# Seven products for eight in the first gate and up block too, with h scaled by x's norm factor

## The chip, the cores and the metric

The kernel runs on one core of one Trainium2 chip. The time is the device time of one execution in microseconds; the median of three runs is given. TensorE multiplies; VectorE (DVE), ScalarE (ACT) and GpSimd (POOL) do the rest; SyncE (SP) and POOL start the DMA transfers. Each engine has a queue of its own, which it works off in the written order.

## The reference

One layer of a hybrid block on 256 rows of width 2048, all in float32:

```
xn = rms_norm(x, norm1_g)
q, k, v, ga, gg = split(xn @ w_in)                 # w_in: 2048 x 5120
att = diff_attention(rope(rms_norm(q)), rope(rms_norm(k)), v)
u   = silu(layer_norm(conv(ga * sigmoid(gg))))
h   = x + concat(att, u) @ w_out                   # w_out: 2048 x 2048
hn  = rms_norm(h, norm2_g)
y   = h + (silu(hn @ w_gate) * (hn @ w_up)) @ w_down   # 2048 x 5632, 5632 x 2048
```

where `rms_norm(t, g) = t * rsqrt(mean(t*t) + 1e-6) * g`.

## The kernel before

**Products.** The 256 rows are two halves of 128 (`m`, `NM = 2`). Every float32 operand is split into a high part (rounded, float32r) and a low part (the rest), and a product is three matmuls: high x high, low x high, high x low. Weights come in chunks of two k-tiles by 512 columns (`raw`, 512 KB). ScalarE rounds a chunk to `whi` (L348), VectorE subtracts to `wlo` (L357); for a chunk marked `by_dma` ScalarE writes `-raw` (L351) and a POOL transfer adds the weights to it (L352). A plain chunk is twelve matmuls of 128x128 by 128x512.

**Seven for eight.** From the second gate and up block on, and in w_down, half of the k-tiles go through a Strassen-like scheme: the two row halves and a pair of weights form a 2x2 problem that takes seven products instead of eight. Such a unit ("s") multiplies one of seven sums of input rows (`forms`: `fhi`, `flo`) with one of seven sums of weights. Its weights are a tile `wb` of 1 MB (`load_pair`); VectorE makes three sums (`pair_sums`, L1064 to L1066), ScalarE rounds (`round_raw` L1071, `round_pair` L1075 and L1076) and VectorE makes the low parts (`split_pair`, L1080 and L1081). A unit "s" is 21 matmuls into the banks Q1 to Q3. The other half of the k-tiles is plain: units "g" (gate) and "u" (up) of twelve matmuls; a capital letter means `by_dma`. A block of 512 columns of gate and up is four "s", four "g" and four "u", in the order of `ORDER` or `FIRST`. Behind the last "s" `bank_sums` puts the products together, and behind the last unit `block_done` finishes the block.

**The first block.** Gate and up block 0 is made of plain chunks (`block`, sixteen chunks, 192 matmuls), with `silu_done` and `up_done` at its end; its inputs are `hT`, h transposed and times norm2's gain, without the factor `rstd2`, which is applied to the sums. During it `make_forms` spreads `rstd2` over a tile (`rep`, two transposes L1000, `rb`), multiplies the transposed rows `hn` by it, and makes the plain parts (`chi`, `clo`) and the forms for all later blocks.

**w_out.** Four column blocks n of 512. The last k-tiles of blocks 0, 1 and 2 are done one after the other, four chunks each, then all eight chunks of block 3, then gate and up block 0. `out_done(n)` adds the result to h (L850), starts the transfer of h to the output, transposes h (L862), scales by the gain (`hn`, L867), splits to `hT` and takes the sum of squares (L524). Blocks 0, 1 and 3 accumulate in the four `acc` banks, block 2 in two `aux` banks; in a Strassen unit Q1, Q6, Q7, Q5 are `acc` and the rest `aux`.

**Order of the work.** The queues' order is written out by the program. `run_chunks` goes through the chunks; ahead of chunk t it issues the splits, sums, roundings and loads of later chunks (splits up to three chunks ahead, sums five, roundings three or four, loads nine; before the first Strassen unit two and three). Generators such as `out_done` and `make_forms` go on by one `yield` at each `resume()`, of which a plain chunk has two and an "s" unit four:

```
until("part", part_of, t + 1 + LO_AHEAD)
...
until("sums", sums_of, t + 1 + ahead - (...), may=may_sum)
...
chunks[t]["multiply"](chunks[t])
```

Pools: `pre`, `once` and `small` hold what is needed until h is done; the pool `ffn` is opened in their place afterwards.

Of the kernel before, what the change touches and what calls it, by code (L numbers as in the profile page):

```python
# [13 lines left out]
F32 = mybir.dt.float32  # L14
# [70 lines left out]
FIRST = "gugusGsUsGsU"  # L85
# [32 lines left out]
def tile_block(  # L118
# [12 lines left out]
    prestack = ExitStack()  # L131
    pre = prestack.enter_context(tc.tile_pool(name="pre", bufs=2))
    once = prestack.enter_context(tc.tile_pool(name="once", bufs=1))
    small = prestack.enter_context(tc.tile_pool(name="small", bufs=4))
# [4 lines left out]
    h = [pre.tile([P, D], F32, tag=f"h{m}", name=f"h{m}", bufs=1) for m in range(NM)]  # L139

    rstd2 = [const.tile([P, 1], F32, tag=f"rstd2_{m}", name=f"rstd2_{m}") for m in range(NM)]
# [3 lines left out]
    neghalf = once.tile([P, 8], F32, tag="neghalf", name="neghalf")  # L145
# [10 lines left out]
    cols = once.tile([P, NR], F32, tag="cols", name="cols")  # L156
# [8 lines left out]
    head = pre.tile([P, NK * N], F32, tag="lod", name="head", bufs=1)[:, : NR + S]  # L165
# [54 lines left out]
    def rsqrt_mean(dst, ss, n, eps):  # L220

        k = dst.shape[-1]
        t = small.tile([P, 8], F32, tag="rsq", name="rsq")
        pool.tensor_scalar(t[:, :k], ss, 1.0 / n, eps, ALU.mult, ALU.add)
        pool.tensor_tensor(dst, t[:, :k], neghalf[:, :k], ALU.pow)

# [114 lines left out]
    def minus_chunk(c):  # L341
        c["lo"] = c["view"](pre.tile([P, NK * N], F32R, tag="lod", name="lod", bufs=1))
        act.activation(c["lo"], c["raw"], AF.Copy, scale=-1.0)
        pool.dma_start(out=c["lo"].rearrange("p k n -> p (k n)"), in_=c["src"].bitcast(F32R), accum_op=ALU.add)
# [174 lines left out]
    rstd1 = [once.tile([P, 1], F32, tag=f"rstd1_{m}", name=f"rstd1_{m}") for m in range(NM)]  # L519
    ss1 = [small.tile([P, D // N], F32, tag=f"ss1_{m}", name=f"ss1_{m}", bufs=1) for m in range(NM)]  # L520

    def square_sum(src, accum, **kw):
        junk = pre.tile([P, N], F32, tag="junk", name="junk", bufs=1)
        act.activation(junk[:, : src.shape[-1]], src, AF.Square, accum_out=accum, **kw)  # L524
# [14 lines left out]
    def x_rest():  # L539
# [6 lines left out]
        for m in range(NM):  # L546
            ss = small.tile([P, 1], F32, tag="ss1", name="ss1")
            dve.tensor_reduce(ss, ss1[m], AX.X, ALU.add)
            rsqrt_mean(rstd1[m], ss, D, EPS)
# [63 lines left out]
    def conv_back(b):  # L613
# [37 lines left out]
        for b in range(2):  # L651
            for t in range(NB // 2):
# [6 lines left out]
                for j in range(2):  # L659
# [3 lines left out]
                    hi = pre.tile([P, S], F32R, tag="mchi", name=f"mchi{ct}", bufs=NCT)  # L663
                    lo = pre.tile([P, S], F32R, tag="mclo", name=f"mclo{ct}", bufs=NCT)
# [137 lines left out]
    def attend_values(hd):  # L802
# [26 lines left out]
        for e in range(2):  # L829
# [3 lines left out]
            pre.tile([P, S], F32R, tag=t, name=t, bufs=4) for t in ("mahi", "malo")) for e in range(2)]  # L833
# [10 lines left out]
    hn = []  # L844
    ss2 = [once.tile([P, 4], F32, tag=f"ss2_{m}", name=f"ss2_{m}") for m in range(NM)]

    def out_done(n, ps):
# [5 lines left out]
        if n == 2:  # L853
            held[0] -= NM
        yield
        for t in range(0, N // P, 2):
# [3 lines left out]
            for i in range(2):  # L860
                for m in range(NM):
                    pe.transpose(pt[:, i, m * P : (m + 1) * P], h[m][:, (k + i) * P : (k + i + 1) * P], ident)  # L862
            if k % HK == 0:
                hn.append(early.tile([P, HK, S], F32, tag="wb", name="hn"))
            rows = hn[k // HK][:, k % HK : k % HK + 2, :]
            for i in range(2):
                act.activation(rows[:, i, :], pt[:, i, :], AF.Copy, scale=col("g2", k + i))  # L867
            hi, lo = lhs_two("h", k)
            act.copy(hi, rows)
            dve.tensor_tensor(lo, rows, hi.bitcast(F32), ALU.subtract)  # L870
            for i in range(2):
                hT[k + i] = (hi[:, i, :], lo[:, i, :])
            yield
        for m in range(NM):
            square_sum(h[m][:, cs], ss2[m][:, n : n + 1])
        if n == D // N - 1:
            yield
            for m in range(NM):
                ss = small.tile([P, 1], F32, tag="ssh", name="ssh")
                dve.tensor_reduce(ss, ss2[m], AX.X, ALU.add)  # L880
                rsqrt_mean(rstd2[m], ss, D, EPS)
            yield
            yield
            prestack.close()
            ffn["pool"] = fp = ctx.enter_context(tc.tile_pool(name="ffn", bufs=1))
            spare_lhs.extend(fp.tile([P, SPARE, 2, S], F32R, tag=f"a{x}", name=f"a{x}") for x in ("hi", "lo"))
            start(make_forms())


    ffn = {}  # L890
    actT = {}
    sil = {}

    def silu_done(ps):
        yield
        for m in range(NM):
            sil[m] = ffn["pool"].tile([P, N], F32, tag=f"sum{m}", name="sil")
            act.activation(sil[m], ps[m], AF.Silu, scale=rstd2[m])

    def up_done(j, ps):  # L900
        fp = ffn["pool"]
        aa = []
        for m in range(NM):
            a = fp.tile([P, N], F32, tag=f"sum{2 + m}", name="a")
            dve.scalar_tensor_tensor(a, ps[m], rstd2[m], sil[m], ALU.mult, ALU.mult)
            aa.append(a)
        yield from lag(2)
        place(0)
        pts = []
        for t in range(NB // 2):  # L910
            pts.append(acc_ps.tile([P, 2, S], F32, tag="acc", name="ps_a"))
            transpose_two(pts[t], aa, t)
        for t in range(NB // 2):
            act.copy(down[0]["at"][j, t][0], pts[t])
        yield
        for t in range(NB // 2):
            hi, lo = down[0]["at"][j, t]
            dve.tensor_tensor(lo, pts[t], hi.bitcast(F32), ALU.subtract)
            down[0]["ready"].add((j, t))
# [10 lines left out]
    def place(g):  # L930
# [6 lines left out]
        free += [tuple(a[:, i] for a in spare_lhs) for i in range(SPARE)]  # L937
        assert len(free) >= len(twos)
# [5 lines left out]
    def transposed(j, aa):  # L944
# [4 lines left out]
        for t in range(N // P // 2):  # L949
# [4 lines left out]
            else:  # L954
                hi, lo = d["at"][j, t]
                if j == FF // N - 1:
                    a = ffn["pool"].tile([P, 2, S], F32, tag=f"sum{2 * t}", name="ac")
# [8 lines left out]
    def pair_forms(j, t, pt):  # L966

        fp = ffn["pool"]
# [22 lines left out]
    def make_forms():  # L991
        fp = ffn["pool"]
        load_pair(chunks[pair_at[0]])
        rep = fp.tile([P, S], F32, tag="sum1", name="rep")
        for m in range(NM):
            act.activation(rep[:, m * P : (m + 1) * P], ident, AF.Identity, bias=rstd2[m], scale=0.0)
        yield from lag(2)
        ps = aux_ps.tile([P, N], F32, tag="aux", name="ps_r")
        for m in range(NM):
            pe.transpose(ps[:, m * P : (m + 1) * P], rep[:, m * P : (m + 1) * P], ident)  # L1000
        yield
        rb = fp.tile([P, S], F32, tag="sum2", name="rb")
        act.copy(rb, ps[:, :S])
        yield
        for i in range(2):
            for k in range(0, HK, 4):
                t = hn[i][:, k : k + 4, :]
                dve.tensor_tensor(t, t, rb.unsqueeze(1).to_broadcast([P, 4, S]), ALU.mult)
                yield from lag(1 if i == 0 else 2)

        nr = HK - NS
        chi = fp.tile([P, 2 * nr, S], F32R, tag="chi", name="chi")
        clo = fp.tile([P, 2 * nr, S], F32R, tag="clo", name="clo")
        for i in range(2):
            act.copy(chi[:, i * nr : (i + 1) * nr], hn[i][:, NS:])
        yield
        pair_sums(chunks[pair_at[0]])
        yield
        for i in range(2):
            dve.tensor_tensor(clo[:, i * nr : (i + 1) * nr], hn[i][:, NS:],  # L1020
                              chi[:, i * nr : (i + 1) * nr].bitcast(F32), ALU.subtract)
            yield from lag(2 - i)
        forms.update(plain={k: (chi[:, i, :], clo[:, i, :]) for i, k in enumerate(REST)})
        a11, a21 = (hn[0][:, :NS, m * P : (m + 1) * P] for m in range(NM))
        a12, a22 = (hn[1][:, :NS, m * P : (m + 1) * P] for m in range(NM))
        fhi = fp.tile([P, 7, NS, P], F32R, tag="fhi", name="fhi")
        flo = fp.tile([P, 7, NS, P], F32R, tag="flo", name="flo")
        f = fp.tile([P, 7, NS, P], F32, tag="wh", name="sums", bufs=2)[:, :4]
# [9 lines left out]
        for i, a in ((0, a11), (1, a12)):  # L1038
            dve.tensor_tensor(flo[:, i], a, fhi[:, i].bitcast(F32), ALU.subtract)
        yield  # L1040
        act.copy(fhi[:, 3:], f)
        round_raw(chunks[pair_at[0]])
        dve.scalar_tensor_tensor(flo[:, 2], a22, -1.0, fhi[:, 2].bitcast(F32), ALU.mult, ALU.subtract)
        yield from lag(2)
        dve.tensor_tensor(flo[:, 3:], f, fhi[:, 3:].bitcast(F32), ALU.subtract)
        forms.update(hi=fhi, lo=flo)

    def load_pair(c):
        if "b" in c:
            return  # L1050
        queue = sp
        if c is chunks[pair_at[0]]:
            c["b"] = ffn["pool"].tile([P, 7, N], F32, tag="wl", name="wb0", bufs=2)[:, :4]
            queue = pool
        else:
            c["b"] = early.tile([P, 4, N], F32, tag="wb", name="wb")
        src = weights([(w, k, col, N) for w, col in c["sides"] for k in c["ks"]])
        queue.dma_start(out=c["b"].rearrange("p k n -> p (k n)"), in_=src)

    def pair_sums(c):  # L1060

        b = c["b"]
        c["t"] = t = ffn["pool"].tile([P, 3, N], F32, tag="wt", name="wt")
# [4 lines left out]
    def round_raw(c):  # L1068
        if "hi" not in c:
            c["hi"] = ffn["pool"].tile([P, 7, N], F32R, tag="wh", name="wh", bufs=2)  # L1070
# [280 lines left out]
```

## Time and profile before

| | |
|---|---|
| three runs | 1035.57, 1035.73, 1035.88 us |
| median | 1035.73 us |
| span of the profiled execution, first to last instruction | 1033.9 us, 1.8 us less than the median of the runs |
| TensorE busy | 1025.0 us (99%) |
| VectorE, ScalarE, POOL busy | 882.0 (85%), 697.5 (67%), 157.1 us (15%) |
| mean granted TensorE clock | 0.999 |
| moved by DMA | 258.05 MB, 250 GB/s on average |

The profiled execution's own time is its span and what lies around it; no figure of its own is given beside the three runs. Times in a timeline are microseconds from the start of the span. Each row has start, length, engine, line of the kernel, operation, "out <- in" with shapes, a count, and in brackets the idle time of the engine before it with what ended it. A matmul's length overlaps the next one's.

### The profile page before, as it was taken

The numbers are of one execution on the slowest core, as the hardware profiler recorded it, in microseconds if no ns is written. First come the engines' busy times: TensorE is split into PE (matmuls) and PEld (weight loads), VectorE is DVE, ScalarE is ACT, GpSimd is POOL, SyncE is SP. The second block draws the span as 40 slices with busy tenths as digits, with TensorE's granted clock in tenths as the row PEclk, the third lists the DMA queues.
The fourth block names the chain that finished last, engine by engine and source line by source line (L and its number), as shares of the span: only waits on it lengthen the run. The fifth ranks groups of instructions, "written<-read, shape, count | busy, mean of one in ns | idle before, by whom it ended". The sixth has DMA issues, their size and how long they took to land.

```text
span 1033.9 us, 13145 instructions
## 1 busy us (share of the span) xinstructions
PE 1025.0 (99%) x4635; PEld 847.3 (82%) x4635; DVE 882.0 (85%) x1111; ACT 697.5 (67%) x933; POOL 157.1 (15%) x198
## 2 busy tenths in 40 slices
PE   9999999999999999999999999999999999999998
PEld 7888887888888888788888888888888888888887
DVE  6699889897646699999989879999898887998984
ACT  7855567857756577787665757776767576767761
POOL 0050332411100101011002120110110221101122
PEclk9999999999999999999999999999999999999999
DMA  9968675676566668798899997987979999889896
GB/s 362 314 202 248 224 208 184 191 217 184 156 211 224 230 241 237 246 325 233 264 291 246 313 267 260 308 249 243 310 239 278 271 263 330 228 257 301 242 259 130
DMA packets 65345, 258.05 MB, mean 250 GB/s; under 512 B 7296, under 2 KB 8576, under 8 KB 57344
## 3 DMA queue, kind: packets, MB, share of 16 engines
q1 hardware_dynamic: 48080, 201.08, 53.6%
q0 software_dynamic: 16768, 55.58, 28.8%
q8 instruction: 36, 0.59, 0.2%
q10 hardware_dynamic: 432, 0.55, 0.2%
q14 instruction: 29, 0.24, 0.1%
HBM read 248.80 MB, written 8.39 MB: 249 GB/s over the span
## 4 chain that ended last, share of the span: by engine, by line
PE 90%; DVE 5%; issue 2%; ACT 2%; POOL 1%; DMA 0%; DVEq 0%
PE q L1120 20%; PE acc L393 11%; PE acc L387 11%; PE acc L388 11%; PE q L1125 10%; PE q L1098 8%; PE q L1100 8%; PE q L1099 8%; DVE wl L1081 1%; PE ps_a L925 1%; DVE wt L1064 1%; DVE wl L1080 1%; ACT whi L348 1%; PE ps_s L734 1%; PE ps_o L812 1%
## 5 line engine op out<-in xcount | busy, mean ns | idle before, releaser
L348 ACT CAST whi<-raw 128x1024 fp32r<-128x1024 f32 (+1 forms) x254 | 261.9, 1041 | 66.0 <-PE acc L388 44.2
L357 DVE TENSOR_TENSOR wlo<-raw,whi 128x1024 fp32r<-128x1024 f32 (+1 forms) x166 | 199.6, 1210 | 41.8 <-ACT whi L348 41.4
L1071 ACT CAST wh<-wb 128x1536 fp32r<-128x1536 f32 x62 | 91.9, 1483 | 117.0 <-issue 67.4
L1080 DVE TENSOR_TENSOR wl<-wb,wh 128x2048 fp32r<-128x2048 f32 x62 | 141.9, 2288 | 33.9 <-ACT wh L1075 33.6
L387 PE MATMUL acc<-whi,lhi 128*128 128x512 f32 x416 | 164.2, 395 | 0.4 <-ACT whi L348 0.4
L388 PE MATMUL acc<-whi,llo 128*128 128x512 f32 x416 | 162.4, 391 | 0.0
L352 POOL DMA_DIRECT2D wlo<-in_wts_dram x74 | 65.2, 881 | 526.6 <-ACT wlo L351 408.1
L1098 PE MATMUL q<-wh,fhi 128*128 128x512 f32 x280 | 109.2, 390 | 1.5 <-DVE sum L1223 1.5
L1100 PE MATMUL q<-wl,fhi 128*128 128x512 f32 x280 | 109.0, 389 | 0.0
L1099 PE MATMUL q<-wh,flo 128*128 128x512 f32 x280 | 109.0, 389 | 0.0
L1081 DVE TENSOR_TENSOR wl<-wt,wh 128x1536 fp32r<-128x1536 f32 x62 | 108.6, 1752 | 0.0
L599 DVE SCALAR_TENSOR_TENSOR y<-upad,cw,y 128x256 f32<-128x256 f32 x240 | 100.7, 484 | 3.4 <-ACT y L592 3.4
L393 PE MATMUL acc<-wlo,lhi 128*128 128x512 f32 x368 | 100.8, 395 | 1.1 <-DVE wlo L357 1.1
L387 PEld LDWEIGHTS acc<-whi,lhi 128*128 128x128 f32 x416 | 78.2, 188 | 17.1 <-ACT whi L348 1.1
L1076 ACT CAST wh<-wt 128x1536 fp32r<-128x1536 f32 x62 | 91.7, 1480 | 0.0
L388 PEld LDWEIGHTS acc<-whi,llo 128*128 128x128 f32 x416 | 78.2, 188 | 16.0
L1125 PE MATMUL q<-wlo,chi 128*128 128x512 f32 x320 | 86.9, 394 | 0.0
L1120 PE MATMUL q<-whi,chi 128*128 128x512 f32 x320 | 85.8, 390 | 0.0
L1120 PE MATMUL q<-whi,clo 128*128 128x512 f32 x320 | 85.7, 390 | 0.0
L393 PEld LDWEIGHTS acc<-wlo,lhi 128*128 128x128 f32 x368 | 68.4, 188 | 15.3 <-DVE wlo L357 1.5
L351 ACT ACTIVATE wlo<-raw 128x1024 fp32r<-128x1024 f32 x74 | 78.0, 1054 | 0.0
L1064 DVE TENSOR_TENSOR wt<-wb 128x1024 f32<-128x1024 f32 x62 | 75.7, 1221 | 1.4 <-DMA wb<-in_wts_dram 0.9
(229 smaller groups left out, 1740.1 us busy)
## 6 DMA issues: line engine op xcount, KB each, us to landing
raw<-in_wts_dram SPq DMA_DIRECT2D x250, 512.0 KB, 6.1
wb<-in_wts_dram SPq DMA_DIRECT2D x61, 1024.0 KB, 7.4
wlo<-in_wts_dram POOLq DMA_DIRECT2D x74, 512.0 KB, 9.2
lod<-in_wts_dram POOLq DMA_DIRECT2D x14, 512.0 KB, 5.9
out_dram<-sum POOLq DMA_DIRECT2D x22, 256.0 KB, 5.9
h<-in_x_dram SPq DMA_DIRECT2D x4, 512.0 KB, 9.6
out_dram<-h POOLq DMA_DIRECT2D x8, 256.0 KB, 3.8
xt<-in_xt_dram SPq DMA_DIRECT2D x6, 256.0 KB, 6.5
```

Of the source, the lines that this page charges most:

```text
L348: act.copy(c["hi"], c["raw"])
L357: dve.tensor_tensor(c["lo"], c["raw"], c["hi"].bitcast(F32), ALU.subtract)
L387: pe.matmul(ps[m], xhi[:, ms], hi[:, j, :], start=c["first"] and j == 0, stop=False)
L388: pe.matmul(ps[m], xlo[:, ms], hi[:, j, :], start=False, stop=False)
L393: pe.matmul(ps[m], xhi[:, ms], lo[:, j, :], start=False, stop=c["last"] and j == nk - 1)
L1080: dve.tensor_tensor(c["lo"][:, 3:], c["b"], c["hi"][:, 3:].bitcast(F32), ALU.subtract)
L1081: dve.tensor_tensor(c["lo"][:, :3], c["t"], c["hi"][:, :3].bitcast(F32), ALU.subtract)
L1098: pe.matmul(ps, fhi[:, f, p, :], c["hi"][:, w], start=bool(first), stop=False)
L1099: pe.matmul(ps, flo[:, f, p, :], c["hi"][:, w], start=False, stop=False)
L1100: pe.matmul(ps, fhi[:, f, p, :], c["lo"][:, w], start=False, stop=bool(last))
L1120: pe.matmul(ps, plain[i][e][:, ms], hi[:, i, ns], stop=False, start=i == e == 0 and bool(c["first"].get(qs[m])))
L1125: pe.matmul(sum_bank(c, qs[m])[:, ns], plain[i][0][:, ms], lo[:, i, ns], start=False, stop=i == 1 and ns.stop == N and bool(c["last"].get( ...
```

## The change

Block 0 becomes a block of units like the others, in a new order `FIRST`; block 1 takes `ORDER`. h is multiplied by `rstd1`, x's norm factor, ahead of the transposes (`scaled`). The forms are made of these scaled rows during w_out's column block 3: column blocks 0 and 2 give the rows `hn` for the forms, 1 and 3 the plain parts. The rest of the norm (`rest` = the norm factor of h over that of x) is applied in the Silu and in the product of gate and up. The pools are cut in another way: one group on the right side of memory is kept until h is done (`latestack`), one pool opens when attention and convolution are through (`open_first`) and one after h (`open_second`); the weight tiles of the pairs alternate between these two pools (`turn`).

```diff
-FIRST = "gugusGsUsGsU"
+FIRST = "sgguusGsGsUu"
...
+            t = rsqrt_mean(rstd1[m], ss, D, EPS)
+            pool.tensor_tensor(rms1[:, m : m + 1], t, rstd1[m], ALU.mult)
...
+    def open_first():
+        while not (len(mixa) == len(mixc) == KD // 2):
+            yield
+        prestack.close()
+        fp = ffn["wt"] = ffn["w", 0] = ctx.enter_context(tc.tile_pool(name="ffn0", bufs=1))
+        ffn["scaled"] = ...
+        ffn["hn"] = early.tile([P, HK, S], F32, tag="wb", name="hn")
...
     def out_done(n, ps):
+        if n == 0:
+            yield from open_first()
+        scaled = ffn["scaled"]
+        for m in range(NM):
+            act.activation(scaled[:, m], h[m][:, cs], AF.Copy, scale=rstd1[m])
         yield
...
+            if n % 2 == 0:
+                rows = ffn["hn"][:, n // 2 * NS + t : n // 2 * NS + t + 2, :]
+                for i in range(2):
+                    act.activation(rows[:, i, :], pt[:, i, :], AF.Copy, scale=col("g2", k + i))
+            else:
+                hi, lo = (a[:, t : t + 2] for a in ffn["plain"][0]) if n == 1 else lhs_two("h", k)
+                for i in range(2):
+                    act.activation(hi[:, i], pt[:, i], AF.Copy, scale=col("g2", k + i))
+                for i in range(2):
+                    dve.scalar_tensor_tensor(lo[:, i], pt[:, i], col("g2", k + i), hi[:, i].bitcast(F32), ...)
+            yield
+        if n == 2:
+            start(make_forms())
...
+                rsqrt_mean(rest[m], ss, D, EPS)
+                pool.tensor_tensor(rest[m], rest[m], rms1[:, m : m + 1], ALU.mult)
+            open_second()
+            yield from lag(2)
+            (two copies of the plain parts out of the arena)
...
     def make_forms():
-        (rep, two transposes, rb; hn times rb; chi and clo; sums of the first pair in between)
+        first = chunks[pair_at[0]]
+        load_pair(first)
+        ...
         (f1, f2; fhi; f3, f0; flo; fhi[3:]; flo[3:]: as before)
+        yield
+        sums_of(pair_at[0])
+        round_raw(first)
+        yield from lag(2)
+        part_of(pair_at[0])
...
     def round_raw(c):
         if "hi" not in c:
+            while ("w", c["turn"]) not in ffn:
+                resume()
+            c["hi"] = ffn["w", c["turn"]].tile([P, 7, N], F32R, tag="wh", name="wh")
...
     def products_done(q):
-            act.activation(t, t, AF.Silu)
+            act.activation(t, t, AF.Silu, scale=rest[m])
     def block_done(j, q):
-            dve.tensor_tensor(u[m], u[m], g[m], ALU.mult)
+            dve.scalar_tensor_tensor(u[m], u[m], rest[m], g[m], ALU.mult, ALU.mult)
...
-            if j:
-                gate_up_block(j, FIRST if j == 1 else ORDER)
-                continue
-            block("w_gate", j * N, range(KD), fh, silu_done)
-            block("w_up", j * N, range(KD), fh, lambda ps, j=j: up_done(j, ps))
+            gate_up_block(j, FIRST if j == 0 else ORDER)
```

183 lines of the change are left out of this document (63 added, 120 removed).

## The prediction

> **What bounds the kernel now.** I read the page first, then who waited for whom on TensorE, then the order in time of TensorE, ScalarE and VectorE from 292 to 432 us, where the changed code runs. In the page, the busy line and the chain by engine:
>
> ```profile
> PE 1025.0 (99%) x4635; PEld 847.3 (82%) x4635; DVE 882.0 (85%) x1111; ACT 697.5 (67%) x933; POOL 157.1 (15%) x198
> PE 90%; DVE 5%; issue 2%; ACT 2%; POOL 1%; DMA 0%; DVEq 0%
> ```
>
> All waits of TensorE (engine, line, what it waited for: us in total, times, longest):
>
> ```profile
> PE q L1098 <- DVE sum L1223: 1.7, 2, 1.5
> PE ps_warm L152 <- POOL neghalf L146: 1.4, 1, 1.4
> PE acc L393 <- DVE wlo L357: 1.1, 1, 1.1
> PE acc L387 <- ACT whi L348: 0.4, 1, 0.4
> PE q L1120 <- DVE alo L962: 0.2, 1, 0.2
> ```
>
> TensorE never stops for more than 1.5 us. So a product less is time won, and any new wait of TensorE is time lost, one for one. What a product costs is its distance to the next, not its 0.39 us of modelled length; the timeline of TensorE (start, us, line, tile, count, idle before):
>
> ```profile
> 336.22 0.39 PE L387 MATMUL acc<-whi,mchi 128*128 128x512 f32 x1
> ...
> 338.94 0.39 PE L387 MATMUL acc<-whi,lhi 128*128 128x512 f32 x1
> ...
> 352.60 1.07 PE L393 MATMUL acc<-wlo,lhi 128*128 128x512 f32 x4
> 353.51 0.38 PE L1000 MATMUL ps_r<-ident,rep 128*128 128x128 f32 x2
> ...
> 355.58 1.08 PE L393 MATMUL acc<-wlo,lhi 128*128 128x512 f32 x4
> ...
> 431.16 0.50 PE L1098 MATMUL q<-wh,fhi 128*128 128x512 f32 x1 [1.53 <-DVE sum L1223]
> ```
>
> A chunk of twelve matmuls runs from 336.22 to 338.94: 2.72 us, 0.227 each. The profiled execution's span is 1033.9 us; the runs' median is 1035.73, so 1.8 us lie around the span, and I carry them over unchanged.
>
> **Gains on TensorE.** (1) The first block falls from 192 matmuls to four units of 21 and eight of 12, 180: -12 x 0.227 = -2.72. (2) The two transposes that spread rstd2 go; with them a chunk took 355.58 - 352.60 = 2.98 instead of 2.72: -0.26. (3) The 1.53 us wait at 431.16 stands at the end of block 1, whose old order ends "sGsU", so the bank sums come one unit before the end. Both new orders end with two units behind the last s, and blocks with that ending show no such wait (the list has only 0.2 us more of it): -1.53, bounds 0 and -1.53. Sum of gains: -4.51.
>
> **What is moved, on ScalarE and VectorE.** The forms for the seven products are now made while w_out's last column block (eight chunks c8 to c1, 316.22 to 338.94) is multiplied, and the first unit s0 of the new block starts right behind c1. Prices, ScalarE first, taken start to start:
>
> ```profile
> 315.51 1.06 ACT L348 CAST whi<-raw 128x1024 fp32r<-128x1024 f32 x1 [0.68 <-PE acc L388]
> 319.58 0.84 ACT L867 ACTIVATE hn<-ps_h,cols 128x256 f32<-128x256 f32 x2 [3.01 <-PE ps_h L862]
> ...
> 321.92 0.83 ACT L867 ACTIVATE hn<-ps_h,cols 128x256 f32<-128x256 f32 x2
> ...
> 323.31 0.63 ACT L524 ACTIVATE junk<-h 128x512 f32<-128x512 f32 x1
> ...
> 324.69 1.98 ACT L348 CAST whi<-raw 128x1024 fp32r<-128x1024 f32 x2
> ...
> 370.35 0.61 ACT L1031 CAST fhi<-hn 128x512 fp32r<-128x512 f32 x1
> ...
> 374.40 1.92 ACT L1041 CAST fhi<-sums 128x2048 fp32r<-128x2048 f32 x1 [1.23 <-DVE sums L1036]
> 376.21 1.47 ACT L1071 CAST wh<-wb 128x1536 fp32r<-128x1536 f32 x1
> ...
> 387.63 0.60 ACT L1075 CAST wh<-wb 128x512 fp32r<-128x512 f32 x1
> 388.13 1.48 ACT L1076 CAST wh<-wt 128x1536 fp32r<-128x1536 f32 x1
> ```
>
> and VectorE:
>
> ```profile
> 313.91 2.36 DVE L357 TENSOR_TENSOR wlo<-raw,whi 128x1024 fp32r<-128x1024 f32 x2 [0.49 <-ACT whi L348]
> 316.19 1.28 DVE L850 TENSOR_TENSOR h<-h,acc 128x512 f32<-128x512 f32 x2
> ...
> 338.69 1.28 DVE L850 TENSOR_TENSOR h<-h,acc 128x512 f32<-128x512 f32 x2 [0.87 <-PE acc L393]
> ...
> 363.48 1.22 DVE L1064 TENSOR_TENSOR wt<-wb 128x1024 f32<-128x1024 f32 x1
> ...
> 366.07 1.22 DVE L1020 TENSOR_TENSOR clo<-hn,chi 128x1024 fp32r<-128x1024 f32 x1
> ...
> 374.28 1.29 DVE L1039 TENSOR_TENSOR flo<-hn,fhi 128x512 fp32r<-128x512 f32 x2
> 375.48 1.22 DVE L357 TENSOR_TENSOR wlo<-raw,whi 128x1024 fp32r<-128x1024 f32 x1
> ...
> 380.94 2.28 DVE L1045 TENSOR_TENSOR flo<-sums,fhi 128x2048 fp32r<-128x2048 f32 x1
> 383.14 1.22 DVE L357 TENSOR_TENSOR wlo<-raw,whi 128x1024 fp32r<-128x1024 f32 x1
> ...
> 388.26 2.29 DVE L1080 TENSOR_TENSOR wl<-wb,wh 128x2048 fp32r<-128x2048 f32 x1 [1.45 <-ACT wh L1075]
> 390.47 1.75 DVE L1081 TENSOR_TENSOR wl<-wt,wh 128x1536 fp32r<-128x1536 f32 x1
> ```
>
> So on VectorE: split of a chunk 1.14; a 128x512 operation 0.60; flo's last four 2.20; the three sums of a weight pair 363.48 to 366.07 = 2.59; the pair's low parts 2.21 and about 1.67. On ScalarE: a rounding 0.95 to 1.05, a 128x512 copy 0.52, fhi's last four 1.81, a pair's roundings 1.38, 0.52 and 1.48, two squares with their reads 324.69 - 323.31 = 1.38.
>
> **The queue of VectorE, walked through.** Every weight chunk gives the waiting generators two steps. The output step of column block 2 takes four of them, so make_forms begins in the middle of c6. Each queue runs in its written order:
> - adds of block 2: 316.19 to 317.47, then the split for c5, to 318.6. The split for c4 waits for its rounding, which stands behind the rows of hn (transposes, 319.58): 321.5 to 322.7.
> - rows done 322.7; forms f1, f2 to 324.1. The split for c3 waits for its rounding behind two squares (322.7 + 1.38 + 1.05): 325.2 to 326.3. f3, f0 to 327.5; split c2 to 328.8; three flo to 330.6; split c1 to 331.8; flo's last four (their fhi ready at 330.4) to 334.0.
> - In the step before c2 comes the whole of s0: three sums to 336.6; ScalarE rounds the first sum (337.3), low parts 337.3 to 341.2.
> - splits of the next three units, 3 x 1.14, to 344.6; then, since sums run five units ahead and the second s stands exactly five behind the first, the second pair's sums, to 347.2. Only then come the adds of column block 3, which are written in the middle of s0: first half done at 347.9.
>
> Before, these adds ran at 338.69. TensorE needs them early: s0's first two products take the two free accumulators, the third (Q7) takes the one that holds block 3's first half. TensorE reaches s0 at 338.94; it waits 0.3 for the first low part, 1.0 for the second (341.3), and Q7, due at 341.6, starts at 347.95: 6.4. **Sum of new waits 7.7.** The later products and transposes find scaled h (349.2) and their bank ready. Bounds: were VectorE never idle from 317.4 on, its 24.6 us of work (five splits 5.7; forms 6.4; s0 6.5; three splits 3.4; sums 2.6) would put the first add's end at 342.6 against 340.3 wanted, 2.3; as walked it is 7.7; with a wait of ScalarE for memory in s0, 9. I take 7.7, since all its links are rows.
>
> Restart: TensorE's longest wait here is 1.5 us and what follows is at full pace; but at the start of the kernel it is slow:
>
> ```profile
> 1.35 3.54 PE L152 MATMUL ps_warm<-ident 128*128 128x128 f32 x17 [1.35 <-POOL neghalf L146]
> ...
> 295.25 0.60 PE L862 MATMUL ps_h<-ident,h 128*128 128x128 f32 x4
> 295.60 0.48 PE L387 MATMUL acc<-whi,mchi 128*128 128x512 f32 x1
> ```
>
> Seventeen transposes took 3.54, where four take 0.35 later (17 would take 1.5): 2.0 lost after a long idle. A 6.4 us wait lies between, so 0 to 2.0; I take the middle, +1.0. The Trainium skill (TensorE: Matmul & The Clock Gate, "What's actually happening") says that the array falls to half clock after at least one idle window of about 3.4 us, and is released after about as long a busy one; by it an estimate of 1.7 would stand in place of 1.0. The trace has no such gap to test it on.
>
> **What I cost at nothing, with its cover.** Scaling h is 2 x 0.52 on ScalarE between the adds (317.47) and the transposes (318.94): done at 318.1. The first new pool lies where attention and convolution had their tiles, all read before column block 0's last products can run. The first pair's load moves from POOL's queue to SP's and is free to go by about 316; the second pair's waits for hn, free at 330.6, and for raw buffers at 331.8:
>
> ```profile
> wb<-in_wts_dram SPq DMA_DIRECT2D x61, 1024.0 KB, 7.4
> ```
>
> it lands near 340, before its sums. Blocks 0 and 1 take four more transfers for low parts (three and one), each a ScalarE pass instead of a VectorE split, in a stretch where TensorE has units of 12 or 21 ahead. The extra POOL operations on one column (two early, two late) lie on an engine that is 15% busy; rest is first used behind the last s of the block. Scaling hn by rb, its split and their copies (VectorE about 7 us in block 0) go from under TensorE's cover, worth nothing to it. The rest of block 0 has cover: s1 starts near 363, its low parts stand at 362.
>
> **Sum.** -4.51 + 7.7 + 1.0 = +4.2: 1033.9 + 4.2 = 1038.1 of span, 1039.9 as time.
>
> **Rivals.**
> A (faster): VectorE reaches the adds in time. Place: Q7 of s0. The seven products pay for themselves by over 0.2% only when the new waits stay under 2.4 us (1035.73 - 4.51 + 2.4 = 1033.6), that is, when the first add ends by 342.7; with no wait it is 1031.2. For it: TensorE was fully covered before, and VectorE was idle for 20 of the 47 us ahead of the new block (stretch, TensorE, its loads, VectorE, ScalarE, POOL):
>
> ```profile
> 292.00:339.00 47.00, 47.00 (x221) 38.87 (x220) 26.94 (x29) 28.97 (x47) 3.31 (x6) 1.00 0.63 213
> ```
>
> Against: the floor of 2.3 above asks for a VectorE that never waits, and the walk has five waits on ScalarE. 0.13.
> B (no change): the second pair's sums stand behind the adds, or the forms come a chunk earlier. The waits fall by 2.6, to 5.1, and Q7's own to 3.8, too short for a slow restart: 1035.73 - 4.51 + 5.1 = 1036.3. 0.16.
> C (slower still): the slow restart in full, or ScalarE held for the memory of the second new pool, which lies under h while its output transfer and POOL's small operations end: 1041 to 1042. 0.21, within slower.
> The forecast itself, 1038 to 1041: 0.50. That the matmuls don't fall by twelve isn't a case: the count is fixed by the units.
>
> Faster by over 0.2% is below 1033.66, slower above 1037.80; 0.2% is about what a measurement of this kernel can tell. Faster 0.13, same 0.16, slower 0.71. The range 1034.0 to 1042.0 leaves out most of A and little of C; the forecast's own is 1038 to 1041.
>
> **What would show it.** After: a wait of TensorE at Q7 of the first unit (its L1098 line) on the adds to h, of some 6 us; two short ones on wl before it; 4.5 us less elsewhere; no 1.5 us wait at the end of block 1. Matmuls at twice their distance behind the wait would show the slow restart. Wrong if the adds to h stand in VectorE's queue ahead of the second pair's sums, if VectorE is not in one piece busy from 331 to 347, or if the first unit's accumulators are all free.

## The result

| | before | after |
|---|---|---|
| median of four runs | 1035.81 us | 1046.44 us (1046.13 to 1046.61) |
| span of the profiled execution | 1033.9 us | 1044.6 us |
| mean granted TensorE clock | 0.999 | 0.995 |

The changed kernel is slower: ratio 1.0102, 95% interval 1.0088 to 1.0116. The forecast was 1039.9 us with a range of 1034.0 to 1042.0, so the direction was right and the size was not: the span grew by 10.7 us where 4.2 were forecast.

The busy line of the page after the change:

```profile
PE 1027.8 (98%) x4621; PEld 847.4 (81%) x4621; DVE 891.6 (85%) x1121; ACT 707.6 (68%) x939; POOL 159.1 (15%) x205
```

TensorE has fourteen matmuls less than before (4635), as forecast, and is busy 2.8 us longer. So part of the loss is in how fast matmuls run, and the rest is waiting. The longest waits of TensorE (what waits, what it waits for: us in total, times, longest):

```profile
PE q L1077 <- DVE h L874: 6.1, 1, 6.1
PE q L1077 <- DVE sum L1188: 2.7, 1, 2.7
...
PE q L1079 <- DVE wl L1059: 0.7, 1, 0.7
PE q L1079 <- DVE wl L1060: 0.7, 1, 0.7
```

The 6.1 us are the forecast wait for the adds to h, and the 0.7 on L1060 is the second low part of s0. The 2.7 us on the bank sums (L1188) and the 0.7 on L1059 were not forecast. The order in time on TensorE shows where they stand, and what matmuls cost behind them (start, length, line, tile, idle time before):

```profile
338.89 0.39 PE L1077 MATMUL q<-wh,fhi 128*128 128x512 f32 x1
...
347.76 0.79 PE L1077 MATMUL q<-wh,fhi 128*128 128x512 f32 x1 [6.09 <-DVE h L874]
348.35 0.63 PE L1078 MATMUL q<-wh,flo 128*128 128x512 f32 x1
348.78 0.63 PE L1079 MATMUL q<-wl,fhi 128*128 128x512 f32 x1
...
351.64 0.39 PE L1078 MATMUL q<-wh,flo 128*128 128x512 f32 x1
...
354.23 1.07 PE L1099 MATMUL q<-whi,chi 128*128 128x512 f32 x4
...
366.45 0.50 PE L1079 MATMUL q<-wl,fhi 128*128 128x512 f32 x1 [0.72 <-DVE wl L1059]
...
394.89 0.50 PE L1077 MATMUL q<-wh,fhi 128*128 128x512 f32 x1 [2.74 <-DVE sum L1188]
...
400.94 1.07 PE L1099 MATMUL q<-whi,chi 128*128 128x512 f32 x4
```

Behind the long wait matmuls stand 348.78 - 348.35 = 0.43 us apart, and 0.39 us long instead of 0.63 again from 351.64 on. The same happens behind the wait at 394.89: the eighteen matmuls that follow to 400.94 take 6.05 us, and 18 x 0.227 = 4.08. The granted clock says the same (a stretch, its length, busy time of TensorE, its loads, VectorE, ScalarE and POOL, then the clock, DMA share and GB/s):

```profile
344.66:351.49 6.83, 3.73 (x11) 3.05 (x12) 3.57 (x5) 1.34 (x2) 1.09 (x2) 0.50 0.81 325
395.86:399.27 3.41, 3.41 (x8) 2.34 (x9) 3.41 (x6) 1.61 (x3) 0.00 (x0) 0.50 0.87 245
```

In these two stretches it was 0.50, and 1.00 in the microsecond on either side of each. The first fall came while TensorE still waited, the second 1 us after it had gone on.

VectorE's queue up to the adds, which the prediction had walked:

```profile
341.03 3.49 DVE L360 TENSOR_TENSOR wlo<-raw,whi 128x1024 fp32r<-128x1024 f32 x3
344.44 1.22 DVE L1041 TENSOR_TENSOR wt<-wb 128x1024 f32<-128x1024 f32 x1
...
347.02 1.28 DVE L874 TENSOR_TENSOR h<-h,acc 128x512 f32<-128x512 f32 x2
```

Three splits, three sums of the second pair, and only then the adds: the walk had this order, and Q7 at 347.95 where it came at 347.76.

What followed was not walked. ScalarE's next pair, and the POOL operations that it waits for:

```profile
357.20 1.06 ACT L354 ACTIVATE wlo<-raw 128x1024 fp32r<-128x1024 f32 x1
362.02 1.48 ACT L1050 CAST wh<-wb 128x1536 fp32r<-128x1536 f32 x1 [3.76 <-POOL rest L915]
```

```profile
358.69 0.93 POOL L355 DMA_DIRECT2D wlo<-in_wts_dram  x1 [9.43 <-ACT wlo L354]
...
361.79 0.19 POOL L915 TENSOR_TENSOR rest<-rest,rms 128x1 f32<-128x1 f32 x1
```

The pair's weight tile lies in the second new pool, on memory of the small tiles, and so it waits until the last small operation, `rest`, is through. That operation stands in POOL's queue behind the transfer for the low part of a chunk, which waits for ScalarE's pass at 357.20. ScalarE stood still for 3.76 us, and the pair's low parts came at 364.10:

```profile
364.10 2.29 DVE L1059 TENSOR_TENSOR wl<-wb,wh 128x2048 fp32r<-128x2048 f32 x1 [7.65 <-ACT wh L1054]
...
378.82 2.29 DVE L1059 TENSOR_TENSOR wl<-wb,wh 128x2048 fp32r<-128x2048 f32 x1 [0.69 <-ACT wh L1054]
...
394.15 0.68 DVE L1188 TENSOR_TENSOR sum<-q,sum 128x512 f32<-128x512 f32 x1
```

From there VectorE needs (378.82 - 364.10) / 2 = 7.36 us a pair. TensorE's s and g together take 33 x 0.227 = 7.48. So nothing that is late here is caught up, and 30 us later the bank sums are late.

**The 10.7 us, from these rows.** Stall in s0: from 338.89 to 347.76 are 8.87 us for six matmuls of 1.36, so 7.5. The slow matmuls behind it: 354.23 - 347.76 = 6.47, against 4.67 in the kernel without a wait shown below, so 1.8. The second s: 0.7 to 0.9. The bank sums: 2.7 of wait and 2.0 of slow matmuls. Against that: fourteen matmuls less, -3.0 (2.72 and 0.26), and the old 1.53 gone. Together 10.2 to 10.4; 0.3 to 0.5 was not traced.

### The profile page after: what moved, and what is told of

It is laid out like the page before. It is cut to its first block, busy times and chain, and to the rows that moved or that the text cites. A ratio compares the mean times of both kernels' runs of the same rounds, so it can differ in the third digit from the quotient of the medians.

```text
span 1044.6 us, 13138 instructions
## 1 busy us (share of the span) xinstructions
PE 1027.8 (98%) x4621; PEld 847.4 (81%) x4621; DVE 891.6 (85%) x1121; ACT 707.6 (68%) x939; POOL 159.1 (15%) x205
## 5 line engine op out<-in xcount | busy, mean ns | idle before, releaser
L360 DVE TENSOR_TENSOR wlo<-raw,whi 128x1024 fp32r<-128x1024 f32 (+1 forms) x154 | 185.2, 1211 | 42.4 <-ACT whi L351 39.0
L1059 DVE TENSOR_TENSOR wl<-wb,wh 128x2048 fp32r<-128x2048 f32 x66 | 151.1, 2289 | 43.0 <-ACT wh L1054 42.6
L390 PE MATMUL acc<-whi,lhi 128*128 128x512 f32 x352 | 139.3, 396 | 0.2 <-ACT whi L351 0.2
L391 PE MATMUL acc<-whi,llo 128*128 128x512 f32 x352 | 137.6, 391 | 0.0
L1077 PE MATMUL q<-wh,fhi 128*128 128x512 f32 x308 | 122.0, 396 | 8.9 <-DVE h L874 6.1
L1079 PE MATMUL q<-wl,fhi 128*128 128x512 f32 x308 | 121.2, 393 | 1.4 <-DVE wl L1059 0.7
L1078 PE MATMUL q<-wh,flo 128*128 128x512 f32 x308 | 121.0, 393 | 0.0
L1060 DVE TENSOR_TENSOR wl<-wt,wh 128x1536 fp32r<-128x1536 f32 x66 | 115.7, 1752 | 0.0
L396 PE MATMUL acc<-wlo,lhi 128*128 128x512 f32 x304 | 83.5, 395 | 0.6 <-DVE wlo L360 0.6
L390 PEld LDWEIGHTS acc<-whi,lhi 128*128 128x128 f32 x352 | 66.4, 189 | 14.2 <-ACT whi L351 0.6
L391 PEld LDWEIGHTS acc<-whi,llo 128*128 128x128 f32 x352 | 66.4, 189 | 13.6
L1077 PEld LDWEIGHTS q<-wh,fhi 128*128 128x128 f32 x308 | 58.4, 190 | 22.5 <-DVE h L874 6.4
```

Of the source, the lines that this page charges most:

```text
L360: dve.tensor_tensor(c["lo"], c["raw"], c["hi"].bitcast(F32), ALU.subtract)
L390: pe.matmul(ps[m], xhi[:, ms], hi[:, j, :], start=c["first"] and j == 0, stop=False)
L391: pe.matmul(ps[m], xlo[:, ms], hi[:, j, :], start=False, stop=False)
L1059: dve.tensor_tensor(c["lo"][:, 3:], c["b"], c["hi"][:, 3:].bitcast(F32), ALU.subtract)
L1060: dve.tensor_tensor(c["lo"][:, :3], c["t"], c["hi"][:, :3].bitcast(F32), ALU.subtract)
L1077: pe.matmul(ps, fhi[:, f, p, :], c["hi"][:, w], start=bool(first), stop=False)
```

## The experiments

In all of them the kernel before ran beside: 1035.93, 1035.64 and 1035.78 us in the three groups (e1 to e4, e5 to e8, e9 and e10). Times below are medians.

**e1: the adds ahead.** Theory: Q7 waits because of the written order of VectorE's queue.

```diff
 def out_done(n, ps):
     ... (adds to h)
+        if n == D // N - 1:
+            yield
 ... (w_out's last column block)
+    chunks[-1]["prompt"] = True
```

> Edit: the adds of w_out's column block 3 to h are written right behind the last w_out chunk, so VectorE's queue has them ahead of the split for the unit three ahead (1.14 us) and of the second pair's sums (2.59), and behind all else as before. Theory (queue order): in the changed kernel these adds run at 347.02 because of what stands ahead of them, and the third product of the first unit waits for them; here they start near 343.3, so that wait falls from 6.1 to about 2.5 us and, being shorter than the waits after which the clock fell to half (6.1 and 2.7), costs no slow matmuls: -3.7 and -2.0, together 1040.7 us (1040 to 1041.5). The wait at the end of block 0 (2.7 us on the bank sums, with 1.9 of slow clock) stays. Rival 1 (the second wait is only the echo of the first): it goes too, about 1036. Rival 2 (the first unit waits for something other than these adds): no change, 1046.4.

Measured: 1041.86 us, ratio 1.0057 (1.0041 to 1.0072). VectorE and TensorE around Q7:

```profile
340.88 2.35 DVE L360 TENSOR_TENSOR wlo<-raw,whi 128x1024 fp32r<-128x1024 f32 x2
343.15 1.28 DVE L874 TENSOR_TENSOR h<-h,acc 128x512 f32<-128x512 f32 x2
```

```profile
343.89 0.80 PE L1079 MATMUL q<-wh,fhi 128*128 128x512 f32 x1 [2.37 <-DVE h L874]
344.48 0.63 PE L1080 MATMUL q<-wh,flo 128*128 128x512 f32 x1
```

The adds moved ahead of one split and the three sums, and the wait fell from 6.09 to 2.37 us. So the first long wait was the order of the queue. But the matmuls behind a wait of only 2.37 us are slow as well (0.43 apart), which is why the time came out 1.2 us above what was expected. The wait on the bank sums stayed (2.8 us): it is a thing of its own.

**e2 and e6: the small tiles kept.** Theory: the second pair is held for memory of small tiles that POOL still works on, and the late bank sums follow from that. The last sums of squares and roots are put in a pool that is never closed, so the second new pool no longer lies on them.

```diff
-    vectors = latestack.enter_context(tc.tile_pool(name="vectors", ...))
-    once = latestack.enter_context(tc.tile_pool(name="once", ...))
+    vectors = ctx.enter_context(tc.tile_pool(name="vectors", ...))
+    once = ctx.enter_context(tc.tile_pool(name="once", ...))
...
-                ss = small.tile([P, 1], F32, tag="ssh", name="ssh")
+                ss = once.tile([P, 1], F32, tag=f"ssh{m}", name="ssh")
-                rsqrt_mean(rest[m], ss, D, EPS)
+                rsqrt_mean(rest[m], ss, D, EPS, once, f"rsq{m}")
```

To make room, `cols`, `rstd1` and three other small tiles went from the kept pools to `late` in e2 and to `small` in e6, where also 32 bytes were added to the kept pool, so that the tiles of `late` begin where they did.

> Edit: the small tiles that POOL reads while it makes the rest of the norm (neghalf, rms1, the sums of squares and their scratch) are in pools that stay open, so the second new pool's first tile does not wait for POOL; the other small vectors move to the pool of h. Theory (memory hold): in the changed kernel ScalarE stands 3.76 us ahead of the second pair's first rounding (362.02), until POOL's last operation on rest; with four pairs close together VectorE never wins that back, and the bank sums of block 0 come 2.7 us late. Here the rounding runs near 358.2, the 0.7 us wait at 366.45 goes and the one at 394.89 falls to under 0.5 with its slow clock: -5.3, 1041.1 us (1040.5 to 1042.5). The 6.1 us wait stays. Rival (order of units): the new order has pairs at units 5, 7, 9 and 12, and VectorE needs 7.36 us a pair for 7.48 us of products, so it is late anyway: only the 0.7 goes, 1045.5. Rival (echo of the first wait): no change, 1046.4.

> Edit: the small pools kept open as in the run with that edit alone, now padded so that the tiles of h and of the mixed rows begin at a multiple of 64 bytes. Nothing else. Theory: in that run 1.3 us were lost before 335 us by the shift of these tiles by 32 bytes and not by the order of anything; here w_out's matmuls stand at 0.227 us again, the first unit starts at 338.9 instead of 340.3, and the rest is as there: 1.3 us less, 1041.1 us by the profiled span. Rival (the 1.3 us came from the pools' order of opening or from POOL): it stays.

Measured: e2 1043.91 us, ratio 1.0077 (1.0063 to 1.0091); e6 1043.07 us, 1.0072 (1.0059 to 1.0086). In e6, ScalarE at the place of the 3.76 us, VectorE's low parts of that pair and its first bank sum, and TensorE's waits:

```profile
358.40 1.06 ACT L355 ACTIVATE wlo<-raw 128x1024 fp32r<-128x1024 f32 x1
359.37 1.46 ACT L1051 CAST wh<-wb 128x1536 fp32r<-128x1536 f32 x1
```

```profile
361.43 2.29 DVE L1060 TENSOR_TENSOR wl<-wb,wh 128x2048 fp32r<-128x2048 f32 x1 [3.49 <-POOL rsq L227]
...
391.48 0.68 DVE L1189 TENSOR_TENSOR sum<-q,sum 128x512 f32<-128x512 f32 x1
```

```profile
PE q L1078 <- DVE h L875: 6.1, 1, 6.1
...
PE q L1078 <- DVE sum L1192: 0.4, 1, 0.4
```

The rounding follows at once. The bracket at 361.43 names an operation of POOL that had ended at 361.08 (360.89 + 0.19); the rounding that these low parts take, ScalarE's next one, ended at 361.34 (360.73 + 0.61), and that is what they waited for. The low parts come 2.67 us earlier (361.43 for 364.10), and so does the first bank sum, 30 us later (391.48 for 394.15): in between nothing was caught up in either kernel. The 0.7 us wait of the second s is gone, and the wait on the bank sums falls from 2.74 to 0.4 us, while the 6.1 us stay. So nearly all of the lateness of the bank sums was caused by the memory of the second pool, not by the stall of s0. Both kernels are some 2 to 3 us slower than expected; in e6 one part that can be read is a longer slow stretch behind the 6.1 us wait, whose matmuls are 0.43 apart until 354.06 (until 351.64 in the changed kernel):

```profile
353.64 0.58 PE L1079 MATMUL q<-wh,flo 128*128 128x512 f32 x1
354.06 0.39 PE L1080 MATMUL q<-wl,fhi 128*128 128x512 f32 x1
```

With it, from Q7 to the next unit are 7.06 us in e6 (348.36 to 355.42) and 6.47 in the changed kernel, and s0 starts 0.6 us later (339.49 for 338.89): together 1.2 us. The rest of the difference was not traced.

What the hold cost can be read from these two traces. From the first matmul of s1 to the first one behind the last s are 35.83 us in the changed kernel (365.11 to 400.94) and 30.95 in e6 (366.32 to 397.27): 4.9 us less.

**e3: the gap filled.** The changed kernel with 60 transposes of TensorE where it would wait for Q7. Nothing is gained by them; they tell whether slow matmuls follow from idling.

```diff
             if n in (1, 3, 5):
                 resume()
+            if n == 1 and c is chunks[pair_at[0]]:
+                warm_up(60)
```

> Edit: between the second and third product of the first unit TensorE does 60 transposes of the identity (about 5.3 us at full pace) into a bank that nobody reads, inside the 6.1 us in which it waits. Theory (clock): the matmuls behind that wait stood at twice their distance (0.43 for 0.227 us) from 347.76 to 351.2 and the granted clock was 0.50 from 345 to 350, because TensorE stood idle; with work in the gap the clock stays at 1.00 there and 1.5 to 2.0 us go: 1044.6 us (1044.2 to 1045.2). Rival (the slow matmuls have another cause, such as their operands or banks): no change or, if the transposes push the rest back, more than 1046.4.

Measured: 1044.55 us, ratio 1.0084 (1.0070 to 1.0098), granted clock 1.000 in the profiled execution.

```profile
342.38 6.71 PE L154 MATMUL ps_warm<-ident 128*128 128x128 f32 x60
348.84 0.48 PE L1077 MATMUL q<-wh,fhi 128*128 128x512 f32 x1
349.16 0.39 PE L1078 MATMUL q<-wh,flo 128*128 128x512 f32 x1
349.39 0.40 PE L1079 MATMUL q<-wl,fhi 128*128 128x512 f32 x1
...
353.63 1.08 PE L1101 MATMUL q<-whi,chi 128*128 128x512 f32 x4
...
399.35 1.07 PE L1101 MATMUL q<-whi,chi 128*128 128x512 f32 x4
```

The matmuls behind are at full pace, 0.23 apart, and the kernel is 1.9 us faster than the change. So idle time of TensorE makes the slow stretch, not the operands or the banks.

That the time came out as expected is in part luck. The transposes took 342.38 to 348.84 = 6.46 us and not 5.3, Q7 started 1.1 us later, and at the next unit only 0.6 us were won (353.63 for 354.23). Another 1.0 came at the end of block 0 (399.35 for 400.94), where nothing was edited: there TensorE waited 2.71 us (2.74 in the changed kernel), and this time the clock stayed at 1.00.

**e4, e5, e8: both causes taken away.** e4 joins e1 and e2 and also moves the splits of the second and third unit behind the adds (s0 is the first unit). e5 keeps the pools as in e6, and moves the splits of the third and fourth unit and the second pair's sums one unit later still. e8 in addition makes the first pair's sums as soon as f1 and f2 are made, before the other forms.

```diff
 (e5)
-                until("part", part_of, t + 1 + LO_AHEAD)
+                until("part", part_of, t + 1 + LO_AHEAD if t > first else first + 1 + (t == first))
-                ahead = SUMS_AHEAD if t >= first else 0
+                ahead = SUMS_AHEAD if t > first else 4 if t == first else 0
 (e8, in make_forms behind f1, f2)
+        pair_sums(first)
```

> Edit: adds written right behind the last w_out chunk; the splits for the second and third units wait until after them; and the small pools kept open. Theory: VectorE reaches the adds at 341.1, behind the first unit's low parts; the third product waits under 0.5 us, no clock falls, the holds further on go. Left: 0.15 + 0.86 on the first unit's low parts. Of the 10.6 us that the changed kernel lost, 13.9 with its gains, 13 come back: 1032.7 us (1032 to 1034.5), 0.3% faster than the kernel before. Rival (order of units is the cause at the end of block 0): 1036 to 1037.5. Rival (VectorE and ScalarE simply have too much work from 316 to 400): a new wait of 2 us or more elsewhere, 1035 or above.

Measured: 1040.71 us, ratio 1.0045 (1.0032 to 1.0058). Q7 no longer waits, but a new wait takes its place, in the last product of s0:

```profile
350.64 0.76 PE L1079 MATMUL q<-wh,fhi 128*128 128x512 f32 x1 [3.29 <-DVE llo L903]
```

```profile
343.63 3.49 DVE L360 TENSOR_TENSOR wlo<-raw,whi 128x1024 fp32r<-128x1024 f32 x3
347.04 1.22 DVE L1043 TENSOR_TENSOR wt<-wb 128x1024 f32<-128x1024 f32 x1
...
349.62 1.65 DVE L903 SCALAR_TENSOR_TENSOR llo<-ps_h,cols,lhi 128x256 fp32r<-128x256 f32 x4
```

The low parts of the transposed h, which clear the transposes' bank for that product, now stood behind the same splits and sums. The queue was full; one entry had only changed places with another.

> Edit: as the run with both edits, but VectorE's queue has, behind the adds of column block 3, only one split ahead of the low parts of h's transposed rows; the splits of the third and fourth unit and the second pair's sums come behind them; and the kept pools are padded so that the tiles of h and of the mixed rows begin at a multiple of 64 bytes again. Theory: what was left in the run with both edits was a wait of 3.3 us of the first unit's seventh product on those low parts (llo), queued behind three splits and the sums, with 1.7 us of slow clock behind it, and 1.3 us lost before 335 us, where the matmuls stood at 0.233 instead of 0.227 us while the rows' tiles began at an odd multiple of 32 bytes. All of it goes: span 1031, time 1032.7 us (1032.0 to 1034.0), 0.3% faster than the kernel before. Rival (VectorE and ScalarE have too much to do from 316 to 400): a new wait of 1.5 us or more shows up behind it and the time stays above 1034.5.

> Edit: as the reordered kernel, and the first pair's three weight sums are written right behind the first two row sums, while the last w_out chunks are multiplied, where VectorE stood idle. Theory: then VectorE has no wait of 0.7 us on the first sum's rounding, the first unit's low parts are there at 339.3 where TensorE wants them from 339.35 on, and the two short waits (0.15 and 0.86 us) go too: span 1030, time 1031.7 us (1031.2 to 1033.0), 1.0 less than the reordered kernel. Rival (the first unit's low parts are late because VectorE is short of time, not because it waits): same as the reordered kernel.

Measured: e5 1036.31 us, ratio 1.0008 (0.9999 to 1.0017); e8 1034.36 us, ratio 0.9989 (0.9980 to 0.9997). In e8 VectorE reaches the adds 8 us earlier than in the change, and s0 runs through without a wait (VectorE, then TensorE):

```profile
338.90 1.28 DVE L875 TENSOR_TENSOR h<-h,acc 128x512 f32<-128x512 f32 x2
```

```profile
339.87 0.39 PE L1081 MATMUL q<-wh,fhi 128*128 128x512 f32 x1
...
344.54 1.08 PE L1103 MATMUL q<-whi,chi 128*128 128x512 f32 x4
```

From Q7 to the next unit are 344.54 - 339.87 = 4.67 us. e5, expected at 1032.7, is level with the kernel before: its interval includes 1. e8 is the first version that is faster, by 1.3 us or 0.1%, with an interval that ends just below 1; that is less than the 0.2% which the prediction took for what a measurement can tell. It was expected at 1031.7; its waits show what is missing:

```profile
PE q L1081 <- DVE sum L1192: 1.5, 1, 1.5
...
PE q L1081 <- DVE sum L1195: 0.4, 1, 0.4
PE ps_a L935 <- DVE llo L973: 0.3, 1, 0.3
```

The end of block 0 still waits 1.9 us in all for the bank sums, as block 1 did before the change (1.53). TensorE comes there 10.9 us earlier than in e6 (the last matmul ahead of the wait at 381.05 for 391.93), VectorE's first bank sum only 9.25 us earlier (382.23 for 391.48).

**e9: the bank sums first.** e8, with the next block's pair sums put one unit later.

```diff
-                ahead = SUMS_AHEAD if t > first else 4 if t == first else 0
+                ahead = 4 if t in (first, first + 10) else SUMS_AHEAD if t > first else 0
```

> The version with the early first sums, and one more edit: at the end of block 0 the sums of the next block's second pair (three instructions of VectorE, 1.23 + 0.69 + 0.69 us) are issued one unit later, so that the bank sums stand in front of them in VectorE's queue. Theory (the wait at the end of a block is the order of VectorE's queue): the waits of 1.53 and 0.41 us on the bank sums go, nothing is late behind them, because the pair moved back is not multiplied for 8 us: about 1034.4 - 1.9 = 1032.5 us. Rival 1 (the moved pair sums make the next rounding and its low parts late, since ScalarE rounds them behind the two 0.7 us Silu): a wait of 1 to 2 us on `wl` in block 1 takes the place: 1033.5 to 1034.5. Rival 2 (the bank sums wait for the copy of the first bank on ScalarE, which ended at 378.95, and not for VectorE's queue): no more than 0.7 us comes back, 1033.7.

Measured: 1034.59 us, ratio 0.9989 (0.9980 to 0.9998): the same as e8. Both waits went, and one of 2.02 us came, in the last product of the same unit. It needs the bank that the block's last sums read, and these now stand behind the moved pair sums:

```profile
385.77 0.69 DVE L1047 TENSOR_TENSOR wb<-wt,wb 128x512 f32<-128x512 f32 x1
386.38 1.28 DVE L1211 TENSOR_TENSOR sum<-q,sum 128x512 f32<-128x512 f32 x2
```

```profile
387.12 0.50 PE L1081 MATMUL q<-wh,fhi 128*128 128x512 f32 x1 [2.02 <-DVE sum L1211]
```

None of the three theories had this. VectorE has no hole from 373 to 398 us in this kernel; what is put ahead of one thing there delays another.

**e7 and e10: where tiles begin in memory.** In e2 and e4 w_out's last chunks ran 1.1 us slower than in the other kernels, all matmuls with the mixed rows `mchi`, `mclo` being some 0.006 us further apart. By the addresses of the build, which no trace shows, those tiles began 32 bytes past a multiple of 64. e7 is the kernel before with an unused tile of 32 bytes ahead of the identity, lhi and llo (x's rows) in their pool. Whether it also moved the pools behind, as its expectation took it, no trace shows:

```diff
+    const.tile([P, 8], F32, tag="pad", name="pad")
```

> Edit: the kernel before with one unused tile of 32 bytes ahead of the tiles of TensorE's operands, so that nearly all of them begin at 32 modulo 64 bytes. Theory (alignment): every matmul of 512 columns stands at 0.233 instead of 0.227 us, about 4000 of them, +25 us, 1061 us (1050 to 1070). Rival (only the position against some larger unit, or only the order in memory, mattered): within 2 us of 1036.

Measured: 1035.39 us, ratio 1.0000 (0.9990 to 1.0010): nothing. e10 is e9 without the 32 bytes in the kept pool, so that every tile of `late` is shifted, as in e2 and e4:

> The same kernel as the run before it, without the 32 bytes of padding in the kept pool, so that w_out's mixed rows `mahi`, `malo`, `mchi`, `mclo` and h begin 32 bytes past a multiple of 64, as they did in the two versions with kept pools that were late before 335 us. Theory (where these tiles begin in memory sets the 0.233 in place of 0.227 us from matmul to matmul over w_out's last chunks): about 1.1 us slower than the run before it, 1033.6. Rival (it was the column scales and other small tiles that those versions kept in `late`, or chance): no difference, 1032.5.

Measured: 1035.97 us, ratio 1.0001 (0.9992 to 1.0010), against 1034.59 for e9 in the same group. Groups of TensorE by line between 280 and 338 us, e9 and e10 (busy, mean ns):

```profile
L391 PE MATMUL acc<-whi,mchi 128*128 128x512 f32 x64 | 25.1, 393 | 0.0
```

```profile
L390 PE MATMUL acc<-whi,mchi 128*128 128x512 f32 x62 | 24.7, 398 | 0.0
```

The first unit starts at 339.94 in place of 338.68. So in this kernel the shift of that pool does cost 1.1 to 1.3 us, and for x's rows the same shift costs nothing. Why one and not the other stays open; the shift also moves h and every small tile of the pool. The medians, 1.4 us apart, are no clean measure of it: behind a wait of 2.03 us e10's trace has 3.41 us at a clock of 0.50 (389.04 to 392.45), and e9's, behind 2.02 us, has none.

## Why the prediction was wrong

**Right.** The gains on TensorE by count (4635 to 4621 matmuls). The place, the cause and the size of the first wait: 7.7 us forecast, 7.5 measured, with the order of VectorE's queue as its cause (e1). The old 1.53 us wait of block 1 is gone.

**Wrong, the first step: "The rest of block 0 has cover: s1 starts near 363, its low parts stand at 362."** s1 started at 365.11 and its low parts began at 364.10. The step took memory for granted: it priced POOL's new operations on one column at nothing because POOL is 15% busy, where their place in POOL's queue counted, behind a transfer that waits for ScalarE. By the rows, POOL's six operations take 2.29 us (359.69 to 361.98) and their input was there at 356.44; an estimate from these is that, started then, they would have ended at 358.7, 0.5 us behind ScalarE's pass (358.26) instead of 3.76. No run changed this order alone; e6 takes the whole hold away. It cost 0.7 to 0.9 us at once, and, because a pair on VectorE takes 7.36 us where TensorE gives 7.48, 2.7 us and a second slow stretch of 2.0 us at the end of the block: 5.5 us. e6 shows it: with those tiles out of the way the bank sums are 0.4 us late and 4.9 of the 5.5 us come back; the rest are short waits on the bank sums, which e6 has too. Rival C named the hold for the second pool, but put it inside s0 and at 1.3 us; it was one unit later.

With this step went a part of gain (3): "blocks with that ending show no such wait". That was read from later blocks of the kernel before. Block 0 has the same ending and waited 2.7 us; even with all of e8's edits it waits 1.9, so the ending alone is not what kept those blocks free.

**Wrong, the second step: the restart, "I take the middle, +1.0".** It measured 1.8 behind Q7 (2.4 in e6, from 7.06, and 1.5 in e1, where Q7 to the next unit are 350.04 - 343.89 = 6.15) and came a second time, 2.0, behind a wait that the prediction didn't have. Rival B held a wait of 3.8 us for too short to bring it; in e1 2.37 us were enough. The bound of 2.0 was also read a little high: it took 17 transposes for 1.5 us, and in e3 sixty in a row took 6.46 us at a clock of 1.00, 0.108 each, so 1.8 for seventeen. By the Trainium skill (TensorE: Matmul & The Clock Gate, "What's actually happening") the estimate was 1.7, which the 1.8 behind Q7 bears out better than the middle that I took.

Together: 0.8 for the larger first restart, 5.5 for the second pool, less 0.2 for the first wait, is 6.1 of the 6.5 us by which the forecast was short.

## What to carry to other kernels

When tiles are taken out of a pool that closes, ask which small operation touches the old memory last and what stands ahead of that operation on its own queue; that the engine was only 15% busy did not show it here. When an engine's loop for one unit is as long as the bound engine's unit (7.36 against 7.48 us here), count any delay of it as lasting to the next meeting point, and look at that point for the price. A wait of the bound engine that is removed by moving work in a full queue can come back elsewhere (3.3 us in e4, 2.0 in e9), unless what is moved back is not needed soon (e5). Faster than the kernel before it became only when work was done earlier, in a hole of the queue (e8).

## What the runs showed of the hardware

How long TensorE idled didn't settle whether matmuls ran slow behind it. Slow matmuls followed waits of 2.03 (e10), 2.37 and 2.75 (e1), 2.74 and 6.09 (after) and 3.29 us (e4); full pace followed waits of 1.53 (before), 2.02 (e9) and, in e3, 2.71 us. The slow stretch ended 3.9 us behind the long wait in the changed kernel (347.76 to 351.64) and 5.7 behind it in e6 (348.36 to 354.06), with the same 6.09 us of waiting.

In these traces the granted clock changed on a raster of 3.41 us. In the changed kernel it fell at 344.66 and 395.86 and came back at 351.49 and 399.27; the steps between these, 6.83, 44.37 and 3.41 us, are 2, 13 and 1 times 3.41. Half clock lasted 3.41 us in e1, e4 and e10, and three times as long in e6 (a row as above):

```profile
343.80:354.04 10.24, 5.68 (x15) 4.55 (x16) 5.91 (x9) 2.17 (x4) 1.09 (x2) 0.50 0.70 256
```

In the 3.41 us ahead of each fall TensorE had been busy for 0.3 (e4) to 1.4 us (e10), and in those ahead of each return for 3.0 (e1) to 3.4 us. In e6, where it was busy for 2.27 us from 347.21 to 350.63, the clock stayed at 0.50 for one more step. So a wait's price seems to hang on how it lies on the raster: waits of 2.02 and 2.03 us came out on different sides. That is argued and not shown, since a trace without a change of clock, like e9's at that place, doesn't show where its raster lies. The Trainium skill (TensorE: Matmul & The Clock Gate, "What's actually happening") says that activity is counted in windows of about 3.4 us that run on freely, which agrees with the raster; its condition of one idle window of that length does not agree, since waits shorter than a window were enough in four kernels.

The weight tile that lay on the memory of a tile still in use held up its writer without a line of its own in the list of TensorE's waits: it showed as idle time of ScalarE, released by POOL (3.76 us), and on TensorE only as a late low part and a late sum of VectorE.

Shifting the pool of w_out's mixed rows by 32 bytes went with 188 matmuls that were 1.1 us slower in three kernels (e2, e4, e10); shifting x's rows by as much changed nothing in e7.
